# Queries and keys of retention and of two attention groups: seven block products instead of a plain product, and group-norm roots on VectorE

## The chip, the cores and the metric

The kernel runs on one core of a Trainium2 chip. The metric is the device time of one launch in microseconds. The core has TensorE (PE, matmuls out of SBUF into the eight banks of PSUM), VectorE (DVE), ScalarE (ACT), GpSimd (POOL) and SyncE (SP); SP, ACT and POOL also issue DMAs. Each engine takes its instructions in an order that is fixed when the kernel is built, and waits on semaphores for the others.

## The reference

Two decoder layers on x of 512 tokens x 1024 channels, float32. Each has a mixer and a SwiGLU feed-forward part (FFN), each followed by `x <- LayerNorm(ALPHA * x + sublayer(x))`. The mixer multiplies x by one wide matrix and splits the result:

```python
z = jnp.einsum('bsd,dc->bsc', x, w_in) + b_in
q_a, k_a, v_a, q_r, k_r, v_r, g_r, gate_a, gate_b = jnp.split(z, SPLIT_POINTS, axis=-1)
```

Attention: three groups of six heads with 64 channels, each group with its own window and dilation; scores, a position bias, a softmax, values, and a mix of the groups by their softmax denominators. Retention: four heads with queries and keys of 256 channels and values and gates of 512. Queries and keys are turned by a rotary table, and the output is normalised per token and head:

```python
return jnp.concatenate([t1 * cos - t2 * sin, t1 * sin + t2 * cos], axis=-1)   # rot(t)
return (o - mu) * lax.rsqrt(var + GN_EPS)                                      # after the scan
```

The retention output is multiplied by `silu(g_r)`; both branches are projected, weighted by sigmoid gates, summed and projected again.

## The kernel before

**Numbers in two parts.** Every float32 operand of a matmul is split into a high part (a cast on ScalarE) and a low part (the rest, a subtraction on VectorE): `hilo`, line 92. A product is then three matmuls (`mm3`, line 84): high x high, high x low, low x high. x lies transposed as `xh`, `xl` (1024 channels on 8 x 128 partitions, 512 tokens). A weight tile of 128 x 1024 is loaded into one of 8 `raw` tiles and split into `whi` and `wlo`, four of each.

**Two ways to multiply by x.** The plain way (`wstat`, line 233) holds 128 weight columns still and streams all 512 tokens: 8 x 3 matmuls of 512 columns for a result of 128 channels x 512 tokens, in one bank. The other way is a block scheme with seven products instead of eight (Winograd's form of Strassen). x is cut into channel halves and token halves, and its four sums S1 to S4 are made once per layer in `xs` (`x_sums`, line 185). Two weight matrices of equal shape stand side by side as B (columns 1 and 2, channel halves 1 and 2). Sums of B's blocks are made on the way: P1 = B11 + B12 and P3 = B12 + B22 by an accumulating DMA of POOL's queue (line 321), P2 and P4 by an addition on VectorE (line 347). `Right` (line 306) loads, sums and splits B's blocks product by product. Two routines run the seven products: `tall` (line 377; tokens on partitions, weights stream) and `wide` (line 406; channels on partitions, 256 tokens stream). In `wide` a product is 2 x 4 x 3 matmuls of 256 columns, and its results collect in three chains, a bank each: A for products 1, 6, 7 and 4, C for 5 and 3, X for 2. A function `ev` takes what is done out of the bank: after products 1, 5 and 6 a copy, after 2, 7 and 3 a sum or difference of copy and bank on VectorE, after 4 the bank itself. The FFN and the sigmoid gates use `wide`; values of attention and values with gates of retention use `tall`; queries and keys of both use the plain way.

**Order of work in a layer.** Attention has three steps `hp` (a pair of heads of each group). Step 0 makes its queries and keys along with the arrival of x. For hp = 1 and 2 a stage makes queries and keys of the three groups by `wstat` (lines 811 to 816); `qk_put` (line 712) adds the bias, scales, and writes them into a tile of the pool `opp` (nine slots), for groups 1 and 2 with the tokens reordered by dilation. Then come `rotary(0)`, the values and gates of retention head 0, and for heads 1 to 3 one after the other `rotary(h)` and `ret_values_gates(h)`. After that the sigmoid gates and the projections.

**Side work.** Small pieces of other work sit in the queue `side`. Each `mm3` of the main work gives it credit (`tick`; 0.68 for 512 columns, half of that for 256), and `pace(n)` sets the rate so that what is in the queue would be done in a credit of n. `drain` issues the rest at once. In the stage of hp the attention blocks of hp - 1 are the side work (`attention_pair`, line 513: scores, exponential, transposes, values; a block holds two banks from its scores to the copies of its values, and work tiles of a pool of six), paced to 32. In `rotary(h)` it is the outputs of head h - 1 (`ret_outputs`, line 856), in the values of h the scores of h (`ret_scores`, line 836).

**A retention head.** `rotary` (line 657) makes queries, then keys: four weight units, four banks; VectorE multiplies each bank plus bias by cos and by sin (line 668), adds and subtracts (672, 673), and `hilo` writes four tiles. `ret_outputs` takes four token blocks: matmuls, mean and variance on VectorE (868, 869), the root by `rstd_of` (line 120: a power on GpSimd and a Newton step on VectorE), a subtraction with gating (872), a scaling on ScalarE (873), then `turn`, which transposes the block and stores it.

**What sets the order.** The planner of the tile framework orders the instructions of each engine by the program's order and its own estimates: what is not ready by these is overtaken by what is, as far as free tiles and banks allow.

The functions that the change touches:

Of the kernel before, what the change touches and what calls it, by code (L numbers as in the profile page):

```python
# [12 lines left out]
F32R = mybir.dt.float32r  # L13
AF = mybir.ActivationFunctionType
# [39 lines left out]
def hybrid_kernel(ctx, tc, x, rel_bias, w_in, b_in, w_attn_proj, w_ret_proj, w_out,  # L54
# [65 lines left out]
    def rstd_of(var):  # L120
# [7 lines left out]
        dve.tensor_tensor(out=y, in0=y, in1=t, op=ALU.mult)  # L128
        return y
# [176 lines left out]
    class Right:  # L306
# [319 lines left out]
    bTs, braws = [], []  # L626
    for ly in range(DEPTH):
        bTs.append(sm.tile([P, COLS // P], F32, tag="bT", name="bT", bufs=2))
        braws.append(work("braw")[:COLS // P, :P])

    def bias_cols(ly):
# [3 lines left out]
        dve.tensor_copy(bTs[ly], px[:, :n])  # L635

    def layer(ly, cp):
# [18 lines left out]

        def rotary(h):

            rot = []
            for c0 in (C_QR + h * RQ, C_KR + h * RQ):  # L660
                us = pair_units(w_l, c0)
                prod = []
                for t in range(2):
                    ps = wstat(us, t)
                    pr = []
                    for tb in (cos, sin):
                        m = work("rp")
                        dve.scalar_tensor_tensor(out=m, in0=ps, scalar=bcol(c0 + t * P), in1=tb, op0=ALU.add, op1=ALU.mult)
                        pr.append(m)
                    prod.append(pr)  # L670
                (t1c, t1s), (t2c, t2s) = prod
                dve.tensor_tensor(out=t1c, in0=t1c, in1=t2s, op=ALU.subtract)
                dve.tensor_tensor(out=t1s, in0=t1s, in1=t2c, op=ALU.add)
                pair = []
                for src in (t1c, t1s):
                    o_ = slot("rot")
                    hilo(src, o_[:, 0], o_[:, 1])
                    pair.append(o_)
                rot.append(pair)
            heads[h]["q"], heads[h]["k"] = rot  # L680

        def ret_values_gates(h):
            cv, cg = C_VR + h * RV, C_GR + h * RV
            vr = heads[h]["v"] = [None] * NI
            gs = heads[h]["g"] = [None] * NI
            pairs = {}
# [7 lines left out]
            def gate(i, t):  # L694
                if i // 2 not in pairs:
                    pairs[i // 2] = slot("gs", F32)
                gs[i] = pairs[i // 2][:, i % 2]
# [4 lines left out]
        with stage("attn") as ap_, stage("attw", 4) as aw:  # L702
# [9 lines left out]
            def qk_put(hp, g, j, ps):  # L712
# [5 lines left out]
                dve.tensor_scalar(o_, i_, bcol(cc), (HD ** -0.5, 1.0)[j], op0=ALU.add, op1=ALU.mult)  # L718

# [115 lines left out]
        with stage("ret") as rp:  # L835
            def ret_scores(h):
# [5 lines left out]
                def one(j):  # L842
                    n = S - j * P
                    ps = psum()[:, :n]
                    for d in range(2):
                        k_, q_ = heads[h]["k"][d], heads[h]["q"][d]
                        mm3(ps, k_[:, 0, j * P:(j + 1) * P], k_[:, 1, j * P:(j + 1) * P],
                            q_[:, 0, j * P:], q_[:, 1, j * P:], d == 0, d == 1)
# [7 lines left out]
            def ret_outputs(h):  # L856

                ys = {}

                def one(i):  # L860
# [6 lines left out]
                    mv = sm.tile([P, 2], F32, tag="mv", name="mv")  # L867
                    dve.bn_stats(out=st, in_=po)
                    dve.bn_aggr(out=mv, in_=st)
                    rs = rstd_of(mv[:, 1:2])  # L870
# [335 lines left out]
```

## Time and profile before

| | |
|---|---|
| median of three runs | 2186.73 us (2182.38 to 2186.76) |
| profiled execution | 2185.52 us, span 2183.7 us |
| granted TensorE clock | 0.997 |
| busy: PE, DVE, ACT, POOL | 2161.5, 1396.0, 980.6, 228.3 us |
| DMA | 338.60 MB, 155 GB/s on average |
| attention stages hp = 1 and 2, layer 0 | about 106 to 203 us of the span |
| retention heads 1 and 2 (rotary and values), layer 0 | about 302 to 449 us |

The profile is of one execution, whose own time is 1.8 us longer than its span. A line such as `L82 PE MATMUL ps<-xs,whi 128*128 128x256 f32 x1792 | 325.7, 283 | 0.0` names the line of the kernel, engine, operation, what is written and read, the shape and the count, then the busy time in us, the mean ns of one and the idle time before them with what ended it. Matmuls overlap, so the mean of one is longer than the distance between two. `wlo` and `whi` are the parts of weights, `ps` and `px` banks, `sn` a copy of a bank.

### The profile page before, as it was taken

To read this page: it belongs to the slowest core of one execution; us is meant where nothing else is said; L and a number is where in the kernel's file an instruction comes from. 1 tells how busy PE (TensorE), PEld (TensorE's weight loads), DVE (VectorE), ACT (ScalarE), POOL (GpSimd) and SP (SyncE) were. 2 spreads that over 40 slices of the span, in tenths; PEclk is the share of its full clock that TensorE was granted. 3 is DMA by queue.
4 is the path that set the end of the run, shared out by engine and by line. 5 is a ranking of instruction groups with operands and counts; after the bars stand their busy time and mean duration, and the time that the engine had idled before them with its cause. 6 is when DMAs were issued, how large, how long until landed. Compare 5 with 4: busy or idle time off the path is not lost.

```text
span 2183.7 us, 32442 instructions
## 1 busy us (share of the span) xinstructions
PE 2161.5 (99%) x12906; PEld 1902.4 (87%) x12906; DVE 1396.0 (64%) x2011; ACT 980.6 (45%) x1585; POOL 228.3 (10%) x253
## 2 busy tenths in 40 slices
PE   8999999999999999999999999999999999999998
PEld 7977788889988899989898778888899889999996
DVE  5643677777755685747675346767877447766575
ACT  4444544546633263525245445444556233544350
POOL 4100011011000100010020000111010001000001
PEclk9999999999999999999999999999999999999999
DMA  8944266458685356656269343565577762666551
GB/s 230 235 134 104 59 164 164 135 131 194 190 305 192 88 154 132 171 133 158 93 163 255 89 92 92 140 178 148 137 188 227 260 193 58 175 151 161 125 161 39
DMA packets 304954, 338.60 MB, mean 155 GB/s; under 512 B 21790, under 2 KB 243138, under 8 KB 304673
## 3 DMA queue, kind: packets, MB, share of 16 engines
q1 hardware_dynamic: 227712, 248.81, 37.8%
q0 software_dynamic: 49808, 74.90, 18.1%
q10 hardware_dynamic: 27280, 12.80, 2.1%
q8 instruction: 101, 1.65, 0.3%
q14 instruction: 53, 0.43, 0.1%
HBM read 310.67 MB, written 28.53 MB: 155 GB/s over the span
## 4 chain that ended last, share of the span: by engine, by line
PE 90%; issue 4%; DMA 3%; DVE 2%; POOL 1%; ACT 0%; SPq 0%; POOLq 0%; DVEq 0%; ACTq 0%
PE ps L82 81%; PE px L82 7%; DMA raw<-in_w_in 2%; PE px L546 1%; DMA exd<-wb 1%; PE px L878 1%; POOL ry L125 0%; DMA mb<-exd 0%; DMA exd<-pk 0%; PE px L170 0%; DVE xtok L1001 0%; DVE wlo L336 0%; ACT whi L330 0%; PE px L602 0%; DVE xtok L1010 0%
## 5 line engine op out<-in xcount | busy, mean ns | idle before, releaser
L336 DVE TENSOR_TENSOR wlo<-raw,whi 128x1024 fp32r<-128x1024 f32 (+1 forms) x364 | 417.9, 1150 | 214.1 <-ACT whi L330 212.9
L82 PE MATMUL ps<-xh,whi 128*128 128x256 f32 (+1 forms) x1536 | 516.6, 338 | 4.5 <-ACT whi L93 3.5
L330 ACT CAST whi<-raw 128x1024 fp32r<-128x1024 f32 (+1 forms) x364 | 359.0, 990 | 345.4 <-PE ps L82 205.3
L82 PE MATMUL ps<-xh,wlo 128*128 128x256 f32 (+1 forms) x1536 | 500.9, 327 | 1.0 <-DVE wlo L94 1.0
L82 PE MATMUL ps<-xl,whi 128*128 128x256 f32 (+1 forms) x1536 | 501.2, 327 | 0.2 <-DVE xl L94 0.2
L82 PE MATMUL ps<-xs,whi 128*128 128x256 f32 (+1 forms) x2048 | 404.6, 296 | 0.0
L82 PEld LDWEIGHTS ps<-xs,whi 128*128 128x128 f32 x2048 | 327.7, 191 | 10.3
L94 DVE TENSOR_TENSOR wlo<-raw,whi 128x1024 fp32r<-128x1024 f32 (+2 forms) x162 | 193.3, 1196 | 202.0 <-ACT whi L93 201.0
L82 PEld LDWEIGHTS ps<-xh,whi 128*128 128x128 f32 x1536 | 292.4, 191 | 34.3 <-issue 5.7
L82 PEld LDWEIGHTS ps<-xh,wlo 128*128 128x128 f32 x1536 | 292.9, 191 | 26.5 <-DVE wlo L94 1.2
L82 PEld LDWEIGHTS ps<-xl,whi 128*128 128x128 f32 x1536 | 293.7, 191 | 19.5 <-DVE xl L94 1.0
L82 PE MATMUL ps<-xs,wlo 128*128 128x256 f32 (+1 forms) x1024 | 303.4, 296 | 0.0
L93 ACT CAST whi<-raw 128x1024 fp32r<-128x1024 f32 (+2 forms) x162 | 166.0, 1027 | 240.8 <-PE ps L82 150.7
L82 PE MATMUL ps<-whi,xs 128*128 128x512 f32 (+1 forms) x768 | 219.6, 360 | 0.6 <-ACT whi L330 0.4
L82 PEld LDWEIGHTS ps<-xs,wlo 128*128 128x128 f32 x1024 | 196.0, 191 | 5.0
L82 PE MATMUL ps<-whi,ht 128*128 128x512 f32 x576 | 178.4, 389 | 0.0
L82 PEld LDWEIGHTS ps<-whi,xs 128*128 128x128 f32 x768 | 137.7, 188 | 21.1 <-ACT sn L466 1.0
L82 PE MATMUL ps<-wlo,xs 128*128 128x512 f32 (+1 forms) x384 | 138.1, 360 | 0.8 <-DVE wlo L336 0.8
L321 POOL DMA_DIRECT2D raw<-in_w_in x64 | 79.2, 1263 | 472.9 <-DMA raw<-in_w_in 159.8
L82 PEld LDWEIGHTS ps<-whi,ht 128*128 128x128 f32 x576 | 108.2, 188 | 22.3
L321 POOL DMA_DIRECT2D raw<-in_w_ffn_gate x40 | 51.8, 1295 | 679.4 <-DMA raw<-in_w_ffn_up 251.4
L347 DVE TENSOR_TENSOR raw<-raw 128x1024 f32<-128x1024 f32 (+1 forms) x104 | 119.5, 1149 | 2.7 <-DMA raw<-in_w_in 0.5
(183 smaller groups left out, 2897.0 us busy)
## 6 DMA issues: line engine op xcount, KB each, us to landing
raw<-in_w_in SPq DMA_DIRECT2D x152, 512.0 KB, 4.3
raw<-in_w_ffn_up SPq DMA_DIRECT2D x64, 512.0 KB, 4.1
raw<-in_w_in POOLq DMA_DIRECT2D x48, 512.0 KB, 6.9
raw<-in_w_ffn_gate SPq DMA_DIRECT2D x44, 512.0 KB, 4.6
raw<-in_w_ffn_down SPq DMA_DIRECT2D x44, 512.0 KB, 4.2
raw<-in_w_ffn_gate POOLq DMA_DIRECT2D x40, 512.0 KB, 6.7
raw<-in_w_in SPq DMA_DIRECT2D x72, 256.0 KB, 4.9
raw<-in_w_ret_proj SPq DMA_DIRECT2D x32, 512.0 KB, 6.1
```

The costliest lines, as they stand in the source:

```text
L82: pe.matmul(ps, lhsT=a, rhs=b, start=start, stop=stop, skip_group_check=True)
L93: act.copy(out=hi, in_=src)
L94: dve.tensor_tensor(out=lo, in0=src, in1=hi.bitcast(F32), op=ALU.subtract)
L321: pool.dma_start(r, self.src({"P1": "B12", "P3": "B22"}[n], u), accum_op=ALU.add)
L330: act.copy(out=h, in_=src)
L336: dve.tensor_tensor(out=l, in0=src, in1=h.bitcast(F32), op=ALU.subtract)
L347: dve.tensor_tensor(out=r, in0=r, in1=self.t["B22" if n == "P2" else "B21", u], op=ALU.add)
L546: pe.transpose(px[:, (2 + j) * P:(3 + j) * P], s[:, hh, j * P:(j + 1) * P], ident)
L878: pe.transpose(px[:, t * P:(t + 1) * P], ys[i][:, t * P:(t + 1) * P], ident)
```

## The change

Three parts.

1. **Retention heads 1 to 3.** `rotary` uses one `wide` call: the queries' 256 columns are B's first half, the keys' the second. `biased_copy` (ScalarE, two pieces of 256 tokens, with the bias) takes out products 1, 5, 6 (negated) and 4; VectorE joins after 2, 7 and 3. `turned` multiplies a half of 256 tokens by sin and cos, adds and subtracts, and `hilo` writes it. The four rotary tiles now hold a high or a low part each and are taken from the pool at the start, as are the two of the gates. Head 0 stays plain.
2. **Group-norm roots.** The four blocks of a head collect their variances in one tile, and `rstd_vector` makes the four roots at once on VectorE (a first guess from the number's bits, three Newton steps, twelve instructions); the power on GpSimd is gone from here. The blocks' matmuls and the roots stay in the rotary of the next head (`pace(18)`), the transposes move to that head's values, in front of its scores.
3. **Attention, hp = 1 and 2.** Group 2's queries and keys come first, the plain way; then `qk_group` makes those of groups 0 and 1 in one `wide` call (B's halves: queries and keys of both groups). Its loads are split in two pieces, as the columns lie apart, and so are its accumulating DMAs. ScalarE, not VectorE, adds the bias and writes into the tiles, with the queries' bias scaled beforehand (`bQs`).

```diff
     def load(src, a, b):
         v = view(raw(), a, b)
-        nc.sync.dma_start(v, src)
+        for v_, s_ in pieces(v, src):
+            nc.sync.dma_start(v_, s_)
         return v
+
+    def pieces(v, src):
+        if len(src.shape) == 3:
+            return [(v, src)]
+        n = src.shape[3]
+        return [(v[:, :, g * n:(g + 1) * n], src[:, :, g]) for g in range(src.shape[2])]
...
+    def rstd_vector(var, n):
+        ve, y, t, u = (sm.tile([P, n], F32, tag=f"nr{i}", name="nr", bufs=2) for i in range(4))
+        dve.tensor_scalar(ve, var, EPS, None, op0=ALU.add)
+        dve.tensor_scalar(y.bitcast(I32), ve.bitcast(I32), -0.5, 1597463007.0, op0=ALU.mult, op1=ALU.add)
+        dve.tensor_scalar(ve, ve, -0.5, None, op0=ALU.mult)
+        for _ in range(3):
+            dve.tensor_tensor(out=t, in0=y, in1=y, op=ALU.mult)
+            dve.tensor_tensor(out=u, in0=t, in1=ve, op=ALU.mult)
+            dve.scalar_tensor_tensor(out=y, in0=u, scalar=1.5, in1=y, op0=ALU.add, op1=ALU.mult)
+        return y
...
                     if n in ("P1", "P3"):
-                        pool.dma_start(r, self.src({"P1": "B12", "P3": "B22"}[n], u), accum_op=ALU.add)
+                        for r_, s_ in pieces(r, self.src({"P1": "B12", "P3": "B22"}[n], u)):
+                            pool.dma_start(r_, s_, accum_op=ALU.add)
...
+        def turned(t, ts_, hi, lo):
+            n = t.shape[2]
+            s = view(work("rs"), 2, n)
+            cs, sn_ = (a[:, ts_].unsqueeze(1).to_broadcast([P, 2, n]) for a in (cos, sin))
+            dve.tensor_tensor(out=s, in0=t, in1=sn_, op=ALU.mult)
+            dve.tensor_tensor(out=t, in0=t, in1=cs, op=ALU.mult)
+            dve.tensor_tensor(out=t[:, 0], in0=t[:, 0], in1=s[:, 1], op=ALU.subtract)
+            dve.tensor_tensor(out=t[:, 1], in0=t[:, 1], in1=s[:, 0], op=ALU.add)
+            hilo(t, hi[:, :, ts_], lo[:, :, ts_])
+
         def rotary(h):
+            cq, ck = C_QR + h * RQ, C_KR + h * RQ
+            for n_ in "qk":
+                heads[h][n_] = [slot("rot") for _ in range(2)]
+            if h == 0:
...
+                return
+            sn = {}
+
+            def biased_copy(ps, c, sign=1.0):
+                o_ = view(work("sn"), 2, 256)
+                for q in range(2):
+                    act.activation(out=o_[:, q], in_=ps[:, q * 256:(q + 1) * 256], func=AF.Identity, bias=bcol(c + q * P), scale=sign)
+                return o_
+
+            def ev(i, ps):
+                p2 = ps.rearrange("p (q t) -> p q t", q=2)
+                if i in (1, 5):
+                    sn[i] = biased_copy(ps, cq if i == 1 else ck)
+                elif i == 6:
+                    sn[i] = biased_copy(ps, ck, -1.0)
+                elif i == 2:
+                    dve.tensor_tensor(out=sn[1], in0=p2, in1=sn[1], op=ALU.add)
+                    turned(sn[1], slice(0, 256), *heads[h]["q"])
+                elif i == 7:
+                    dve.tensor_tensor(out=sn[5], in0=sn[5], in1=p2, op=ALU.subtract)
+                    turned(sn[5], slice(256, 512), *heads[h]["k"])
+                elif i == 3:
+                    dve.tensor_tensor(out=sn[6], in0=p2, in1=sn[6], op=ALU.add)
+                    turned(sn[6], slice(0, 256), *heads[h]["k"])
+                elif i == 4:
+                    turned(biased_copy(ps, cq), slice(256, 512), *heads[h]["q"])
+
+            wide(pair_right(w_l[:, :, cq:], w_l[:, :, ck:], 0), x_left, ev)
...
+            def qk_group(hp):
+                def src(b, u):
+                    k = 4 if b[1] == "2" else 0
+                    c = (C_KA if b[2] == "2" else C_QA) + hp * P
+                    return w_l[:, k:k + 4, c:c + 2 * GW].rearrange("p k (g c) -> p k g c", g=2)[:, :, :, :P]
+
+                sn = {}
+
+                def put(v, j, half):
+                    for g in range(2):
...
+                        act.activation(out=o_, in_=i_, func=AF.Identity, bias=bs[:, c:c + 1], scale=(HD ** -0.5, 1.0)[j])
+
+                def ev(i, ps):
+                    p2 = ps.rearrange("p (q t) -> p q t", q=2)
+                    if i in (1, 5, 6):
+                        sn[i] = view(work("sn"), 2, 256)
+                        act.copy(out=sn[i], in_=p2)
+                    elif i == 2:
+                        dve.tensor_tensor(out=sn[1], in0=p2, in1=sn[1], op=ALU.add)
+                        put(sn[1], 0, 0)
...
+                wide(Right(src, [(4, 256)], WIDE, ("B11", "P1", "B22", "P3", "B21")), x_left, ev)
...
                 if hp:
                     for g in range(NG):
+                        qk_slot(hp, g)
+                    for g in range(2, NG):
                         us = qk_units(hp, g)
-                        qk_slot(hp, g)
                         for j in range(2):
                             qk_put(hp, g, j, wstat(us, j))
+                    qk_group(hp)
                     drain()
...
-                    rs = rstd_of(mv[:, 1:2])
...
-                    act.mul(out=y, in_=y, mul=rs)
+                def norms():
+                    rs = rstd_vector(mv[:, :, 1], NI)
+                    for i in range(NI):
+                        act.mul(out=ys[i], in_=ys[i], mul=rs[:, i:i + 1])
...
-                return ops[:1] + n * 2 + ops[1:2] + n * 2 + ops[2:3] + tr[:1] + n * 2 + ops[3:] + tr[1:2] + n * 3 \
-                    + tr[2:3] + n * 4 + tr[3:]
+                return ops[:1] + n * 2 + ops[1:2] + n * 2 + ops[2:3] + n * 3 + ops[3:] + n + [norms] + n, \
+                    n * 2 + tr[:1] + n + tr[1:2] + n + tr[2:3] + n + tr[3:]

             for h in range(RH):
                 if h:
-                    pace(20)
+                    side.extend(ops)
+                    pace(18)
                     rotary(h)
                     drain()
                     vg = ret_values_gates(h)
-                side.extend([nothing] * (8 if h else 1) + ret_scores(h))
+                    side.extend(turns + [nothing] * 2)
+                side.extend([nothing] + ret_scores(h))
                 pace(14 if h == 0 else 30)
                 run(vg)
                 drain()
-                side.extend(ret_outputs(h))
+                ops, turns = ret_outputs(h)
+            side.extend(ops + turns)
```

More of the change, by code (lines that the diff above doesn't have):

```diff
@@ L13 @@
 F32R = mybir.dt.float32r
+I32 = mybir.dt.int32
 AF = mybir.ActivationFunctionType
@@ L635, in bias_cols @@
         dve.tensor_copy(bTs[ly], px[:, :n])
+        act.mul(out=bQs[ly], in_=px[:, C_QA // P:C_QA // P + NQ], mul=HD ** -0.5)
     def layer(ly, cp):
@@ L655, in slot @@
             return opp.tile([P, 2, S], dt, tag="op", name=name)
-        def rotary(h):
[L659 to L680, printed above, removed]
+        def turned(t, ts_, hi, lo):
[7 more added lines that the diff above has]
+            hilo(t, hi[:, :, ts_], lo[:, :, ts_])
@@ L684, in ret_values_gates @@
             vr = heads[h]["v"] = [None] * NI
-            gs = heads[h]["g"] = [None] * NI
-            pairs = {}
+            pairs = [slot("gs", F32) for _ in range(2)]
+            gs = heads[h]["g"] = [pairs[i // 2][:, i % 2] for i in range(NI)]
             def left(i, ps, s):
@@ L858, in ret_outputs @@
                 ys = {}
+                mv = sm.tile([P, NI, 2], F32, tag="mv4", name="mv", bufs=2)
                 def one(i):
```

50 lines of the change are left out of this document (40 added, 10 removed).

## The prediction

> **What bounds the kernel now.** I read the page first: busy shares, then the chain of work that ended last.
>
> ```profile
> PE 2161.5 (99%) x12906; PEld 1902.4 (87%) x12906; DVE 1396.0 (64%) x2011; ACT 980.6 (45%) x1585; POOL 228.3 (10%) x253
> ...
> PE 90%; issue 4%; DMA 3%; DVE 2%; POOL 1%; ACT 0%; SPq 0%; POOLq 0%; DVEq 0%; ACTq 0%
> ```
>
> TensorE is 99% busy and 90% of the chain, so the time is the sum of its matmuls plus a few waits. A busy TensorE row says nothing of the pace, so I took the pace of the two shapes that the change exchanges: the chain inside one retention head (a pure run of 512-column matmuls, the shape of the plain product), and VectorE's timeline and TensorE's row of a stretch in the FFN (pure block products with 256 columns, where the same eviction comes back once per call of `wide`).
>
> ```profile
> 391.13 25.52 PE ps L82 x112
> ```
>
> ```profile
> 857.33 0.69 DVE L1098 TENSOR_TENSOR sn<-ps,sn 128x512 f32<-128x512 f32 x1 [0.65 <-PE ps L82]
> ...
> 877.49 0.69 DVE L1098 TENSOR_TENSOR sn<-ps,sn 128x512 f32<-128x512 f32 x1 [0.65 <-PE ps L82]
> ```
>
> ```profile
> core 0: us, PE busy (x) PEld busy (x) DVE busy (x) ACT busy (x) POOL busy (x), PEclk, DMA share, GB/s
> 877.56:897.72 20.16, 20.16 (x171) 20.16 (x170) 15.14 (x17) 10.90 (x15) 2.56 (x2) 1.00 0.79 183
> 106.00:203.00 97.00, 96.43 (x554) 76.23 (x553) 38.41 (x106) 43.21 (x146) 5.77 (x8) 1.00 0.47 123
> 302.00:449.00 147.00, 147.00 (x678) 122.15 (x677) 106.48 (x163) 68.52 (x94) 15.43 (x19) 1.00 0.58 149
> ```
>
> A 512-column matmul costs 25.52 / 112 = 0.228 us. One call of `wide` takes 877.49 - 857.33 = 20.16 us; by the code it is 7 products x 8 x 3 = 168 matmuls, so 0.120 us each (not half of 0.228). In that stretch TensorE never stopped, with VectorE at 75%. The last two rows are the stages that change: two attention stages (hp = 1 and 2 of layer 0, 48.5 us each: VectorE 40%, ScalarE 45%) and two retention heads (73.5 us each: VectorE 72%).
>
> **What it takes from TensorE.** A plain `rotary` is 2 x 2 x 8 x 3 = 96 matmuls of 512 columns: 96 x 0.228 = 21.88 us. As one `wide` it is 20.16 us, 1.72 less. Two groups' queries and keys in an attention stage are also 96, and also become one `wide`. Heads 1 to 3 of two layers are 6 places, hp = 1 and 2 of two layers are 4: 10 x 1.72 = 17.2 us. Scores, outputs, values and transposes stay the same in number; transposes only move from the next head's rotary to its values.
>
> **What it adds to VectorE in a retention head.** The prices are groups by form; the last is of the heads' window.
>
> ```profile
> L336 DVE TENSOR_TENSOR wlo<-raw,whi 128x1024 fp32r<-128x1024 f32 x308 | 375.8, 1222 | 188.0 <-ACT whi L330 187.2
> ...
> L347 DVE TENSOR_TENSOR raw<-raw 128x1024 f32<-128x1024 f32 x88 | 107.4, 1220 | 1.8
> ...
> L718 DVE TENSOR_SCALAR qk<-ps,bT 128x512 f32<-128x512 f32 x36 | 27.0, 749 | 45.0 <-PE ps L82 44.2
> ...
> L668 DVE SCALAR_TENSOR_TENSOR rp<-ps,bT,cos 128x512 f32<-128x512 f32 x32 | 23.9, 746 | 11.0 <-PE ps L82 11.0
> ...
> L872 DVE SCALAR_TENSOR_TENSOR yb<-px,mv,gs 128x512 f32<-128x512 f32 x32 | 23.7, 740 | 0.0
> ...
> L868 DVE BATCH_NORM_STATS2 st<-px 128x6 f32<-128x512 f32 x32 | 22.2, 693 | 13.9 <-PE px L82 13.9
> L94 DVE TENSOR_TENSOR rot<-rp,rot 128x512 fp32r<-128x512 f32 x32 | 20.8, 676 | 1.9 <-ACT rot L93 1.9
> ...
> L672 DVE TENSOR_TENSOR rp<-rp 128x512 f32<-128x512 f32 x16 | 10.9, 684 | 0.0
> ...
> L126 DVE SCALAR_TENSOR_TENSOR rt<-ry,ve 128x1 f32<-128x1 f32 x48 | 10.4, 219 | 43.1 <-POOL ry L125 42.8
> ...
> L128 DVE TENSOR_TENSOR ry<-ry,rt 128x1 f32<-128x1 f32 x48 | 7.5, 158 | 1.3
> ...
> L127 DVE TENSOR_SCALAR rt<-rt 128x1 f32<-128x1 f32 x48 | 7.2, 151 | 1.2
> ...
> L850 DVE TENSOR_TENSOR pt<-px,dec 128x256 f32<-128x256 f32 x8 | 3.3, 415 | 0.0
> ...
> L869 DVE BATCH_NORM_AGGREGATE mv<-st 128x2 f32<-128x6 f32 x7 | 1.3, 179 | 0.2
> ```
>
> Removed: 4 lows x 1.222, 8 bias-and-turn x 0.746, 4 sums x 0.684, 4 lows x 0.676 = 16.3 us. Added: 7 lows x 1.222, 2 sums for P2 and P4 x 1.220, 3 joins x 0.684, and 4 `turned` of 2 x 0.684 + 2 x 0.415 + 0.676 = 2.87: together 8.55 + 2.44 + 2.05 + 11.50 = 24.5 us. Roots: four times 2 x 0.151 + 0.219 + 0.158 = 0.68, that is 2.7 us, go; twelve small ones on four columns come, about 3 x 0.151 + 6 x 0.158 + 3 x 0.219 = 2.1. The Pool power leaves this place, and with it VectorE's waits behind L125; TensorE did not stand in them, so I count them as nothing. Net +7.6 us a head: 53.2 + 7.6 = 60.8 of 71.8 us, 85%, above the 75% at which the FFN runs without a wait.
>
> Inside the rotary it is tighter. VectorE has 24.5 + outputs 4 x (0.693 + 0.179 + 0.740) = 6.4 + roots 2.1 = 33.0 us, while TensorE has 20.16 + 30 output matmuls x 0.228 = 27.0 us: 6.0 us too many. Three things take that up. The values that follow leave VectorE room. The seven weight lows need nothing of the evictions, and run ahead as far as four weight buffers go: the weight casts before them wait mostly for TensorE to give a buffer back (next fence, L330). Most of the 11.5 us of `turned` falls due only with the scores, late in the values. What can be late is the first pair of lows of the values, 2 x 1.222: between 0 (the FFN's stretch) and 2.4 us a head. I take 0.5, nearer the FFN since its order of work is the same: 6 x 0.5 = 3.0 us.
>
> **ScalarE, and the attention stages.**
>
> ```profile
> L330 ACT CAST whi<-raw 128x1024 fp32r<-128x1024 f32 x308 | 321.6, 1048 | 302.4 <-PE ps L82 178.3 <-issue 63.1 <-DVE raw L347 40.7
> ...
> L1096 ACT COPY sn<-ps 128x512 f32<-128x512 f32 x60 | 34.9, 582 | 4.4 <-PE ps L82 4.4
> ...
> L927 ACT ACTIVATE sb<-sn,bT 128x256 f32<-128x256 f32 x32 | 14.5, 500 | 9.4 <-DVE sn L938 7.3 <-DVE sn L941 2.1
> ```
>
> In a rotary ScalarE gains 3 casts and 8 biased copies, 3 x 1.048 + 8 x 0.500 = 7.1 us, to (34.3 + 7.1) / 71.8 = 58%: free. An attention stage loses 4 casts and 4 evictions of VectorE, and gains 7 casts, 3 copies and 8 biased copies: ScalarE + 3 x 1.048 + 3 x 0.582 + 8 x 0.500 = + 8.9, to 30.5 of 46.8 us (65%); VectorE - 4 x 1.222 - 4 x 0.749 + 7 x 1.222 + 2 x 1.220 + 3 x 0.690 = + 5.2, to 52%. No engine is full there; the waits are in the chain of an attention block (scores, exponential, transposes, copies, values), which shares ScalarE's queue with those casts. Two resources get scarce. Of 8 PSUM banks three blocks in flight hold 6, and `wide` holds two chains and for a while a third: 9. Of 6 work tiles the group keeps 3 for sums. And the side work runs by a credit of 10.9 + 19.0 = 29.9 us where it is paced for 32, so about 3 of some 40 entries are left for the `drain` at the end. The largest stall of TensorE in such a stage today is this one (TensorE's timeline, layer 1):
>
> ```profile
> 1277.24 0.40 PE L82 MATMUL ps<-xh,wlo 128*128 128x512 f32 x1
> 1279.63 1.10 PE L82 MATMUL px<-v,sT 128*128 128x64 f32 x8 [2.00 <-ACT sT L547]
> ...
> 1281.03 0.63 PE L82 MATMUL ps<-xl,whi 128*128 128x512 f32 x1
> 1281.46 0.63 PE L82 MATMUL ps<-xh,wlo 128*128 128x512 f32 x1
> ```
>
> ```profile
> 1280.00:1284.00 4.00, 4.00 (x15) 3.24 (x15) 2.76 (x9) 1.27 (x3) 0.00 (x0) 0.58 0.07 3
> ```
>
> ```profile
> PE px L82 <- ACT sT L547: 2.6, 2, 2.0
> PE px L546 <- ACT s L538: 1.6, 1, 1.6
> ```
>
> It lost 1279.63 - 1277.24 - 0.23 = 2.2 us, and then matmuls came every 0.43 us instead of 0.228, at a granted clock of 0.58 over 4 us (second fence): 8 of them in 3.4 us, 1.6 us more, so 3.8 us. The waits over the whole span (third fence: total, times, longest) have it beside only two others behind an attention block, of 0.6 and 1.6 us. So the added wait of an attention stage lies between a gain of 0.9 (a share of that stall goes, 3.8 / 4) and a loss of 3.8 us. I take 1.0, nearer to no change, because three such waits in four stages and two first heads are all there are today: 4.0 us in all.
>
> [...]
>
> **DMA.** Each new place moves 5 loads and 2 accumulating ones of 512 KB instead of 4 loads, 1.5 MB more, 15 MB on 338.
>
> ```profile
> raw<-in_w_in SPq DMA_DIRECT2D x152, 512.0 KB, 4.3
> raw<-in_w_in POOLq DMA_DIRECT2D x48, 512.0 KB, 6.9
> raw<-in_w_in SPq DMA_DIRECT2D x72, 256.0 KB, 4.9
> ```
>
> P1 needs 4.3 + 6.9 = 11.2 us before its cast. Eight raw tiles let it start in the stage before, as in the FFN row above at a DMA share of 0.79; the stages here have 0.47 and 0.58. In the attention the pieces double the issues (10 on SP, 4 on Pool, for 8 on SP). Without cover, `wide`'s second product would wait 11.2 - 2.9 = 8.3 us; I count 0.
>
> **Sum.** - 17.2 + 3.0 + 4.0 = - 10.2 us. The profiled execution took 2185.52 us (span 2183.7), 1.2 under the median 2186.73 and inside the three runs: 2185.5 - 10.2 = 2175.3, I say 2175 us. Its own range is 2169 (no waits added, 2168.3) to 2182.
>
> **Rivals.**
> 1. The attention stages give their part back: blocks wait for banks and ScalarE, each stage takes the 3.8 us or somewhat more, so - 17.2 + 3 + 15 = + 1, or a few us under before: 2182 to 2191. For it: 9 banks wanted of 8, and the chain above. Against: the order of work is made with these limits known, and it can put a block later.
> 2. VectorE becomes the bound of the retention, and the kernel is slower. Place: the change from rotary to values in heads 1 to 3. If the low parts of the values' first weights stay behind the rotary's evictions in VectorE's order, the 6.0 us too many are TensorE's wait at each head: 6 x 6.0 = 36, so 2185.5 - 17.2 + 36 + 4 = 2208 us. It decides from 17.2 / 6 = 2.9 us a head. For it: 33.0 against 27.0 us. Against: 85% over the whole head, and four buffers of lead.
> 3. Narrow matmuls cost exactly half of wide ones in these stages: 168 x 0.114 = 19.2, 2.7 us a place, so 2185.5 - 27.4 + 7 = 2165 us. The FFN's 0.120 speaks against it. [...]
> 4. It doesn't do what it says: P1 comes late in the attention, 4 x 8.3 = 33 us lost, 2208 us again.
>
> **How the numbers follow.** The forecast has 0.52, rival 1 0.22, rival 2 0.15, rival 3 0.05, rival 4 0.06. A measurement of this kernel tells 0.2% (4.4 us) from no change: faster is below 2182.3, slower above 2191.1. Faster: 0.52 + 0.05 + 0.07 of rival 1 = 0.64; same: 0.15 and 0.03 of the milder rivals 2 and 4 = 0.18; slower 0.18. The range from 2167 to 2192 leaves out the slower cases and half of rival 3.
>
> **What would show it.** TensorE: 96 x 10 matmuls of 512 columns become 168 x 10 of 256, 13,626 in all, at 0.120 us. A retention head takes about 72.3 us instead of 73.5, an attention stage about 47.8 instead of 48.5. VectorE's busy time rises by about 6 x 7.6 + 4 x 5.2 = 66 us, ScalarE's by 78. A wait of TensorE for a low part at the start of the values beyond 2.9 us a head would show rival 2; gaps in front of transposes or values of attention, or a `wide` product held by a bank, rival 1; TensorE waiting for the cast of P1, rival 4.

## The result, and the profile after

| | before | after |
|---|---|---|
| median of four runs | 2185.64 us (2182.38 to 2186.76) | 2219.39 us (2214.42 to 2224.22) |
| ratio after / before | | 1.0152, 95% interval 1.0136 to 1.0168 |
| profiled execution, span | 2183.7 us | 2222.3 us |
| mean granted TensorE clock | 0.997 | 0.988 |
| busy: PE, DVE, ACT | 2161.5, 1396.0, 980.6 us | 2164.5, 1450.5, 1049.8 us |

The change makes the kernel 33.8 us slower; forecast was 2175 us, with a range up to 2192 us. The profiled execution of the changed kernel is the longest of its four (2224.22 us), so sums over its trace are larger than the difference of the medians. First the page of the changed kernel: busy times, and the shares of the chain of work that ended last.

```profile
PE 2164.5 (97%) x13626; PEld 1938.9 (87%) x13626; DVE 1450.5 (65%) x2067; ACT 1049.8 (47%) x1709; POOL 245.9 (11%) x249
...
PE 83%; DMA 6%; DVE 4%; issue 4%; ACT 1%; SPq 1%; POOL 0%; POOLq 0%; ACTq 0%; DVEq 0%
```

The 13,626 matmuls are as predicted. But TensorE's share of the span fell from 99% to 97%, its share of the chain from 90% to 83%, and what took its place there is DMA (3% to 6%) and VectorE (2% to 4%). No engine is anywhere near full beside TensorE. So the loss is waiting, not work. The view of TensorE's waits (what it waited for, us in total, times, longest) says where:

```profile
PE px L983 <- ACT yb L978: 18.0, 6, 3.1
PE px L569 <- ACT s L561: 17.3, 4, 6.8
PE px L83 <- ACT sT L570: 6.3, 3, 3.2
```

Before, the largest waits of this kind were 2.6 and 1.6 us in total. Three groups are new or have grown:

- L983, the transposes of a retention head's normed outputs, which the change moved into the next head's values: 6 waits of 3 us, one for each changed head of two layers.
- L569, the transposes of the softmax weights of an attention block: 4 waits, two in each layer.
- the products of those weights with the values: 3 waits, beside the same attention stages.

For sizes by stage I took TensorE's timeline. "Attention" is from the first attention-score matmul to the first retention-score matmul of a layer (stages hp = 1 and 2, head 0's rotary and values), "retention" from there to the first projection matmul, "a head" from the first score matmul of head 1 to that of head 2, layer 0.

| us, layers 0 / 1 | attention | retention | a head |
|---|---|---|---|
| before | 169.3 / 170.2 | 323.9 / 323.8 | 73.5 |
| after | 181.8 / 186.4 | 330.3 / 330.1 | 75.1 |

So attention lost 12.5 and 16.2 us, retention 6.4 and 6.3 us, 41.4 in all; the profiled spans differ by 38.6, so the rest of the kernel is 2.8 us shorter. Both stages were forecast to gain.

**A head's wait, in four timelines of the changed kernel.** Start, duration, engine, line, operation, tiles; a bracket is the idle time before it and what ended it. TensorE, at the start of the values of head 2 of layer 0 and of head 3:

```profile
411.37 0.39 PE L83 MATMUL ps<-whi,xl 128*128 128x512 f32 x1
414.73 0.66 PE L983 MATMUL px<-ident,yb 128*128 128x128 f32 x4 [2.97 <-ACT yb L978]
...
486.45 0.39 PE L83 MATMUL ps<-whi,xl 128*128 128x512 f32 x1
489.95 0.55 PE L983 MATMUL px<-ident,yb 128*128 128x128 f32 x3 [3.11 <-ACT yb L978]
```

VectorE, just before: the first root instruction, one from the middle, and the last of the chain of twelve (`nr`), between others.

```profile
403.01 0.16 DVE L144 TENSOR_SCALAR nr<-mv 128x4 f32<-128x4 f32 x1
403.08 1.22 DVE L359 TENSOR_TENSOR wlo<-raw,whi 128x1024 fp32r<-128x1024 f32 x1
...
406.92 0.16 DVE L149 TENSOR_TENSOR nr<-nr 128x4 f32<-128x4 f32 x1
407.00 1.22 DVE L359 TENSOR_TENSOR wlo<-raw,whi 128x1024 fp32r<-128x1024 f32 x1
...
413.31 0.15 DVE L150 SCALAR_TENSOR_TENSOR nr<-nr 128x4 f32<-128x4 f32 x1
```

ScalarE, which scales the blocks with these roots:

```profile
413.43 0.62 ACT L94 CAST vr<-sn 128x512 fp32r<-128x512 f32 x1 [2.25 <-DVE sn L753]
413.96 2.56 ACT L978 ACTIVATE yb<-yb,nr 128x512 f32<-128x512 f32 x4
```

The twelve instructions are 12 x 0.16 = 1.9 us of work, but each waits for the one before and stands in VectorE's order behind pieces of 0.4 to 1.2 us: the chain took 413.31 + 0.15 - 403.01 = 10.4 us. ScalarE scales the first block from 413.96, and TensorE, whose transposes of it are third in the side work of the values, stands from 411.76 to 414.73. What comes after the transposes in TensorE's order stands behind them.

**An attention stage's two waits.** TensorE in stage hp = 1 of layer 0 (first two rows), and at the end of hp = 2 (last two):

```profile
108.73 0.40 PE L83 MATMUL ps<-xh,wlo 128*128 128x512 f32 x1
113.88 0.86 PE L569 MATMUL px<-ident,s 128*128 128x128 f32 x2 [4.74 <-ACT s L561]
...
213.12 0.40 PE L83 MATMUL ps<-xh,wlo 128*128 128x512 f32 x1
216.70 1.12 PE L83 MATMUL px<-v,sT 128*128 128x64 f32 x4 [3.19 <-ACT sT L570]
```

The first: SP issues the pieces of the block product's weights from 90.67 (two of B11, then P1's first at 92.73), GpSimd the accumulating DMA of P1 from 98.73; ScalarE casts the sum, and VectorE takes the low part, the sum P2, and only then the softmax of the block (`s`, L559). The rows of SP's queue, GpSimd, ScalarE and VectorE:

```profile
90.67 5.68 SPq L112 DMA_DIRECT2D raw<-in_w_in  x6
```

```profile
92.73 0.92 SPq L112 DMA_DIRECT2D raw<-in_w_in  x1
```

```profile
98.73 2.70 POOL L344 DMA_DIRECT2D raw<-in_w_in  x2 [19.13 <-ACT sn L880]
```

```profile
109.53 1.04 ACT L353 CAST whi<-raw 128x1024 fp32r<-128x1024 f32 x1 [9.54 <-DMA raw<-in_w_in]
```

```profile
110.60 1.22 DVE L359 TENSOR_TENSOR wlo<-raw,whi 128x1024 fp32r<-128x1024 f32 x1 [9.66 <-ACT whi L353]
111.86 1.22 DVE L370 TENSOR_TENSOR raw<-raw 128x1024 f32<-128x1024 f32 x1
113.00 0.28 DVE L559 CUSTOM_DVE_ANT_0 s<-px,bias 128x128 f32<-128x128 f32 x1
```

From the first issue to the cast it took 18.9 us, from P1's own first issue 109.53 - 92.73 = 16.8 us. ScalarE and VectorE had been idle for 9.5 us before these. VectorE's softmax at 113.00 has no idle time before it, so it waited for its turn behind the low part and the sum, not for its scores. The DMA view of 92 to 110 us (KB each, median us from issue to landing) has the plain loads at 6.1 us and the accumulating ones at 9.3, against 5.3 for the plain pieces of this size in the same stretch of the kernel before:

```profile
raw<-in_w_in SPq DMA_DIRECT2D x14, 256.0 KB, 6.1
...
raw<-in_w_in POOLq DMA_DIRECT2D x4, 256.0 KB, 9.3
```

The 16 DMA engines were full in that stretch before the change too. These are the queues of the two views, first before, then after (packets, MB, share of 16 engines; packet times are added up, so a share can pass 100%):

```profile
q1 hardware_dynamic: 9630, 5.25, 104.2%
```

```profile
q1 hardware_dynamic: 7841, 4.26, 86.3%
q0 software_dynamic: 1448, 0.72, 31.9%
```

So P1's two steps, load and accumulation, were put where plain loads already took all the engines' time.

And after each of the four stops TensorE runs slow. Four stretches around them, each long enough to hold all of the slow time (busy time and instructions of PE, PEld, DVE, ACT, POOL; granted clock; DMA share; GB/s):

```profile
108.00:120.00 12.00, 7.26 (x24) 4.71 (x23) 7.27 (x17) 5.67 (x18) 0.00 (x0) 0.72 1.10 251
212.00:230.00 18.00, 13.91 (x57) 9.64 (x57) 4.94 (x13) 5.53 (x19) 1.19 (x1) 0.62 0.49 98
1206.00:1220.00 14.00, 7.16 (x24) 4.61 (x24) 7.26 (x17) 6.96 (x19) 1.30 (x1) 0.76 1.09 241
1316.00:1332.00 16.00, 11.19 (x46) 7.85 (x45) 4.80 (x13) 5.10 (x17) 1.19 (x1) 0.68 0.48 93
```

The lost clock is at most 12 x 0.28 + 18 x 0.38 + 14 x 0.24 + 16 x 0.32 = 18.7 us, an upper bound since a part of the slow time lies within the stops. So the bill is - 17.2 saved, + 18.0 + 17.3 + 6.3 of waits, - 4.2 for the waits of this kind that were there before, and + 18.7 at most for the clock: at most 38.9 us, where the profiled executions are 38.6 apart. The lower clock behind two of the heads' waits (338 to 342 us, clock 0.57, and 1440 to 1445, clock 0.66) adds 1.7 us each, and what is counted twice takes something off. So waits and lost clock make up the loss.

### The profile page after: what moved, and what is told of

Same layout as the page of the kernel before. It is cut to its first block, busy times and chain, and to the rows that moved or that the text cites. A ratio compares the mean times of both kernels' runs of the same rounds, so it can differ in the third digit from the quotient of the medians.

```text
span 2222.3 us, 34158 instructions
## 1 busy us (share of the span) xinstructions
PE 2164.5 (97%) x13626; PEld 1938.9 (87%) x13626; DVE 1450.5 (65%) x2067; ACT 1049.8 (47%) x1709; POOL 245.9 (11%) x249
## 4 chain that ended last, share of the span: by engine, by line
PE 83%; DMA 6%; DVE 4%; issue 4%; ACT 1%; SPq 1%; POOL 0%; POOLq 0%; ACTq 0%; DVEq 0%
PE ps L83 74%; PE px L83 7%; DMA raw<-in_w_in 3%; DVE wlo L359 1%; DMA exd<-wb 1%; PE px L569 1%; PE px L983 1%; DMA fa<-exd 1%; DVE rot L95 0%; POOL ry L134 0%; DMA mb<-exd 0%; PE px L192 0%; DVE xtok L1109 0%; ACT whi L94 0%; DMA exd<-pk 0%
## 5 line engine op out<-in xcount | busy, mean ns | idle before, releaser
L359 DVE TENSOR_TENSOR wlo<-raw,whi 128x1024 fp32r<-128x1024 f32 (+1 forms) x434 | 503.5, 1162 | 317.3 <-ACT whi L353 309.6
L353 ACT CAST whi<-raw 128x1024 fp32r<-128x1024 f32 (+1 forms) x434 | 433.4, 1000 | 481.6 <-PE ps L83 263.6
L83 PE MATMUL ps<-xs,whi 128*128 128x256 f32 (+1 forms) x2688 | 526.5, 294 | 0.0
L83 PE MATMUL ps<-xh,whi 128*128 128x256 f32 (+1 forms) x1456 | 456.2, 315 | 4.5 <-ACT whi L94 3.4
L83 PE MATMUL ps<-xh,wlo 128*128 128x256 f32 (+1 forms) x1456 | 444.6, 306 | 1.2 <-DVE wlo L95 1.2
L83 PE MATMUL ps<-xl,whi 128*128 128x256 f32 (+1 forms) x1456 | 445.2, 306 | 0.2 <-DVE xl L95 0.2
L83 PEld LDWEIGHTS ps<-xs,whi 128*128 128x128 f32 x2688 | 428.0, 191 | 14.2 <-issue 2.0
L83 PE MATMUL ps<-xs,wlo 128*128 128x256 f32 (+1 forms) x1344 | 393.8, 293 | 0.0
L83 PEld LDWEIGHTS ps<-xs,wlo 128*128 128x128 f32 x1344 | 257.1, 191 | 5.0
L95 DVE TENSOR_TENSOR wlo<-raw,whi 128x1024 fp32r<-128x1024 f32 (+2 forms) x122 | 144.5, 1186 | 170.1 <-ACT whi L94 170.1
```

What stands on the lines that cost most here:

```text
L83: pe.matmul(ps, lhsT=a, rhs=b, start=start, stop=stop, skip_group_check=True)
L95: dve.tensor_tensor(out=lo, in0=src, in1=hi.bitcast(F32), op=ALU.subtract)
L353: act.copy(out=h, in_=src)
L359: dve.tensor_tensor(out=l, in0=src, in1=h.bitcast(F32), op=ALU.subtract)
```

## The experiments

**Which part loses.** e1 is the changed kernel with the attention's queries and keys plain again; e2 is the kernel before with the attention part alone.

```diff
 e1, from the changed kernel
                     for g in range(NG):
-                        qk_slot(hp, g)
-                    for g in range(2, NG):
                         us = qk_units(hp, g)
+                        qk_slot(hp, g)
...
-                    qk_group(hp)
```

> The change without its attention part (queries and keys of attention made the plain way, as before). Theory: the two parts lose apart from each other, and of the 38.6 us that the span grew, the retention holds about 6.4 a layer (one wait of 3.1 us for the normalised outputs in each of heads 1 to 3, less 1.7 a head of matmul time). Expected: 2185.6 + 13 = 2198 us, with six waits of TensorE for the transposes of the outputs. Rival: the retention stages are slow only because the attention before them ended late and left work in the queues: then this runs at 2176 to 2186 us and the waits are gone.

> The kernel before with the attention part of the change alone (group 2 plain, then groups 0 and 1 in one block product; rotary, roots and outputs as before). Theory: the losses add up, attention holds 12.5 and 16.3 us by the first scores of retention: 2185.6 + 27 = 2213 us, with waits of 3 to 7 us in front of transposes of the exponentials. Rival: it loses only in company with the retention part; then it stays under 2190 us.

Measured: e1 2199.26 us, ratio 1.0059 (1.0042 to 1.0077); e2 2205.96 us, 1.0084 (1.0065 to 1.0102). Over the kernel before on the same chip (2185.75) that is + 13.5 and + 20.2 us, together 33.7 of 33.8: both parts lose, and within the intervals they add up. e2 lost 7 us less than was expected of it, e1 came out as expected. In the waits of TensorE, e1 keeps the six of the transposes, and e2 the four of the attention:

```profile
PE px L981 <- ACT yb L976: 17.9, 6, 3.0
```

```profile
PE px L555 <- ACT s L547: 16.9, 4, 4.9
```

**Is it the order, or VectorE's capacity?** e3 leaves every instruction as it is and puts the first transpose six entries later in the side work of the values.

```diff
 e3, from the changed kernel
-                    n * 2 + tr[:1] + n + tr[1:2] + n + tr[2:3] + n + tr[3:]
+                    n * 8 + tr[:1] + n + tr[1:2] + n + tr[2:3] + n + tr[3:]
```

> The whole change, with the transposes of a head's outputs six empty entries later in the side work of the values (8 instead of 2 ahead of the first). Theory: VectorE is only late with the roots, by some 3 us when the first transpose comes, and has room afterwards; so the waits of 3.1 us go at all six heads and nothing takes their place: 2219.4 - 19 = 2200 us. Rival: VectorE is the bound of the retention head; then the wait goes elsewhere (to low parts of weights), and the time stays at 2214 to 2222 us.

Measured: 2194.22 us, ratio 1.0034 (1.002 to 1.0048), 25.2 us under the changed kernel. All six waits at the transposes are gone, retention takes 319.1 us in both layers, a head 71.9. VectorE's work is the same, so its capacity was not the bound: rival 2's mechanism falls, for TensorE waits for no low part of the values here. That is 6 us better than expected, as not all of the 25.2 us is the heads' (2 x 11.1 us by the stages): the attention is shorter too, 178.6 / 180.6 us, with no edit there. It goes with a higher clock: the mean is 0.992 in the profiled execution of e3 (0.993 in e4 below) and was 0.988; why is open.

**The roots where they were.** e4 takes the roots of each block on GpSimd again, as in the kernel before; the transposes stay where the change put them.

```diff
 e4, from the changed kernel, in one(i) and norms()
+                    rs = rstd_of(mv[:, i, 1:2])
...
+                    act.mul(out=y, in_=y, mul=rs)
...
                 def norms():
-                    rs = rstd_vector(mv[:, :, 1], NI)
-                    for i in range(NI):
-                        act.mul(out=ys[i], in_=ys[i], mul=rs[:, i:i + 1])
+                    pass
```

> The whole change with the roots as before: one a block, the power on GpSimd, each scaled at once, in place of the twelve instructions for four blocks. The transposes stay where the change put them. Theory: the twelve dependent small instructions, spread in VectorE's order among others of 0.4 to 1.2 us, are what is late (10 us from the first to the last); block by block the first root is there long before the first transpose: the six waits shrink under 1 us each, 2219.4 - 15 = 2204 us, less what VectorE loses in waits for GpSimd. Rival: the evictions of the block product alone make VectorE late; then the waits stay at 2 us or more, 2215 to 2225 us.

Measured: 2191.71 us, ratio 1.0024 (1.0014 to 1.0034), 12 us better than expected and again with a shorter attention; the six waits are gone here too, retention 318.9 / 319.0, a head 71.9. So either end of the dependence cures it: earlier roots (e4) or later transposes (e3). What remains above the kernel before is the attention's, 178.1 / 176.5 us:

```profile
PE px L569 <- ACT s L561: 18.1, 4, 6.2
```

e5 to e9 start from e4.

**The retention part alone.** e5 is e4 with the attention plain (the edits of e1 and e4).

> Retention part with the roots as before (one a block, power on GpSimd), attention the plain way. Theory: the losses of the two parts add up (13.5 + 20.2 us measured apart, 33.7 together), so this is the kernel e4_pool_roots (2191.7) less the 20.2 us of the attention part: 2171.5 us, 14 under before, with no wait of TensorE in heads 1 to 3. Rival: the block product's evictions on VectorE eat part of the 1.7 us a head, and it ends at 2180 to 2186 us.

Measured: 2172.86 us against 2182.91, ratio 0.9958 (0.9944 to 0.9972). This beats both kernels. The chain of waits shows a head without a stop, 383.50 - 311.54 = 71.96 us from one run of matmuls to the same run of the next head:

```profile
311.54 11.64 PE ps L83 x71
...
383.50 11.64 PE ps L83 x71
```

Against 73.5 us before that is 1.5 less, where 1.72 was worked out; six places by 1.72 are 10.3 us, and 2182.91 - 2172.86 = 10.05 were measured. By the interval, the gain lies between 6.1 and 12.2 us. The saving on TensorE was right, and so, within that, was its size.

**P1, the first wait of the attention.** e6 leaves the accumulating DMAs of `qk_group` out, and so computes other sums (P1 is B11 alone, P3 is B12 alone); e7 computes what it should, and loads B11 and P1 before group 2's weights.

```diff
 e6, from e4: Right(..., acc=False) for qk_group, and in load()
-                    if n in ("P1", "P3"):
+                    if n in ("P1", "P3") and self.acc:
```

```diff
 e7, from e4, in qk_group and the stage
-                wide(Right(src, [(4, 256)], WIDE, ("B11", "P1", "B22", "P3", "B21")), x_left, ev)
+                right = Right(src, [(4, 256)], WIDE, ("B11", "P1", "B22", "P3", "B21"))
+                right.load("B11", "P1")
+                return lambda: wide(right, x_left, ev)
...
+                    group = qk_group(hp)
                     for g in range(2, NG):
...
-                    qk_group(hp)
+                    group()
```

> The kernel e4_pool_roots, with the accumulating DMAs of the attention's block product left out (P1 is B11 alone, P3 is B12 alone, so these queries and keys are not the reference's); their matmuls, casts and sums all stay. Theory: the first wait of each layer, 4.8 and 6.6 us at the start of stage hp = 1, comes from P1 that lands late (load, then accumulation) and holds up the attention's softmax behind its cast and its sums in the queues of ScalarE and VectorE: it goes, and with it the half clock after it, 2191.7 - 15 = 2177 us; the wait at the end of hp = 2 (4.7 and 3.6 us) stays or shrinks a little. Rival (PSUM banks and work tiles, or ScalarE's load): nothing there changes, and the time stays at 2188 to 2193 us.

> The kernel e4_pool_roots, with the loads of B11 and P1 of the attention's block product issued before those of the third group. Theory: P1 lands about 3 us earlier (four DMA issues on SP of 0.6 to 0.9 us each), the first wait of each layer falls to about 2 and 4 us, 2191.7 - 6 to 9 = 2183 to 2186 us, unless the third group's own weights then come late. Rival (banks, ScalarE): no change, 2188 to 2193 us.

Measured: e6 2178.84 us, 0.9975 (0.9965 to 0.9985); e7 2183.42 us, 1.0002 (0.9992 to 1.0012). TensorE's waits in e6, then in e7:

```profile
PE px L570 <- ACT s L562: 8.9, 2, 4.5
```

```profile
PE px L569 <- ACT s L561: 10.6, 4, 5.4
```

(The expectations' 4.8, 4.7, 6.6 and 3.6 us count from the start of the matmul before each stop; TensorE's idle times in e4 are 4.4, 4.3, 6.2 and 3.2.) In e6 the two first waits are gone and the two at the third pair are left, 4.5 and 4.4 us. In e7 the first ones shrink from 4.4 and 6.2 us to 1.0 and 1.2, with the sums computed in full, and attention takes 172.9 / 169.6 us. Each over the kernel before beside it (2185.75 for e4, 2182.91 for e6 and e7), e4 stands at + 6.0 us, e6 at - 4.1 and e7 at + 0.5: without the accumulations the kernel gains 10.0 us, and moving two loads ahead gives 5.5 of them. So the first wait is P1's lateness. What makes P1 late, the second step or the full DMA engines, these two runs do not separate, since e6 takes away both the step and its traffic.

**Banks.** e8 lets two attention blocks be in flight instead of three, which frees two banks.

```diff
 e8, from e4
-        order = ((0, scores), (2, values), (1, turn)) if hp < 2 else ((1, turn), (0, scores), (1, values))
+        order = ((0, scores), (2, values), (1, turn)) if hp < 0 else ((1, turn), (0, scores), (1, values))
```

> The kernel e4_pool_roots, with the attention blocks of all three steps in the order that the third has already: two blocks in flight instead of three, so 4 banks instead of 6. Theory of late DMAs: the waits of 4.8, 4.7, 6.6 and 3.6 us stay, 2188 to 2196 us (a little more, since less is in flight). Rival (nine banks wanted of eight, and six work tiles): the waits go, and it falls to 2172 to 2180 us.

Measured: 2193.02 us, 1.0049 (1.0034 to 1.0064), + 10.1 us where e4 stands at + 6.0, and the four waits are there:

```profile
PE px L569 <- ACT s L561: 17.2, 4, 7.1
```

This order also has less in flight, so the run alone is not clean. But e6 and e9 (below) leave banks and work tiles as they are, and there the first and the second waits are gone; so neither half of rival 1's reason (nine banks wanted of eight, six work tiles) is a cause by itself.

**The second wait.** At the third pair, TensorE waits for a block whose VectorE and ScalarE queues stand behind the exchange of softmax weights through memory (`exd`, `fa`). In the changed kernel, VectorE's row there, and ScalarE's, whose copy of the weights is what TensorE waited for at 216.70 and stands behind ScalarE's own issue of the read of `fa` (216.00):

```profile
218.33 0.69 DVE L620 TENSOR_TENSOR y<-y,fa 128x512 f32<-128x512 f32 x1 [8.99 <-DMA fa<-exd]
```

```profile
216.38 0.43 ACT L570 COPY sT<-px 128x128 f32<-128x128 f32 x2 [6.35 <-DMA exd<-wb]
```

The DMA views of the kernel before and the changed one: the write of 4 KB took 4.9 us before, and 10.3 after. (In layer 1 it is the read that grew, from 2.9 to 6.9 us.)

```profile
exd<-wb ACTq DMA_DIRECT2D x1, 4.0 KB, 4.9
...
fa<-exd ACTq DMA_DIRECT2D x1, 4.0 KB, 2.6
```

```profile
exd<-wb ACTq DMA_DIRECT2D x1, 4.0 KB, 10.3
```

In that stretch GpSimd's accumulating loads of head 0's values run. Before the change the next of them was issued at 207.79, after the exchange of 200.12 to 207.6; now two are issued at 205.73 and 208.65, beside the write of 205.65. The share of the DMA engines was 0.15 at 200 to 205 us before, and 1.10 at 211 to 216 after. e9 leaves out those of head 0's values and gates, and so computes other values and gates for this head.

```diff
 e9, from e4
             right = halves(w_l, 0, (2, 2), cv, cg, RV)
+            right.acc = h > 0
```

> The kernel e4_pool_roots, with the accumulating DMAs left out in the values and gates of retention head 0 alone (P1 is B11, P3 is B12 there, so that head's values are not the reference's). Theory: the second wait of each layer (4.7 and 3.6 us, where the third attention pair begins) comes from the exchange of softmax weights through memory, whose last small DMA takes 5.6 to 7.4 us because these accumulations run at the same time, where it takes about 3 in the kernel before; VectorE waits for it with the next block's scores behind it. Then it lands in about 3 us, the two waits fall under 2 us, and the time is 2191.7 - 6 to 10 = 2182 to 2186 us; the first waits (4.8 and 6.6) stay. Rival: the exchange begins later for other reasons (more of ScalarE's work ahead of it), and the waits stay at 3 to 5 us: 2188 to 2194 us.

Measured: 2177.99 us against 2182.7, 0.9975 (0.9966 to 0.9985). Read of `fa` in e4, then in e9, and TensorE's waits of e9:

```profile
fa<-exd ACTq DMA_DIRECT2D x1, 4.0 KB, 7.4
```

```profile
fa<-exd ACTq DMA_DIRECT2D x1, 4.0 KB, 2.9
```

```profile
PE px L571 <- ACT s L563: 6.0, 2, 3.8
```

The second waits are gone in both layers, and attention takes 168.7 / 170.4 us. The time is below the range expected, as the first waits shrank as well: they are 2.2 and 3.8 us instead of 4.4 and 6.2, though this edit lies after them; why is open. That the accumulating DMAs and the exchange meet is shown, and that their meeting costs the second wait; which resource they share is not.

**Roots on VectorE, with time to spare.** e10 is the retention part alone with the change's own roots and e3's later transposes.

> Retention part alone with the roots on VectorE as changed, and the transposes six entries later. Theory: where nothing waits for the roots, their place costs little: 2199.3 - 25 (what the same edit gave in the whole change) = 2174 us, within 3 us of e5_ret_pool (2172.9). Rival: the twelve small instructions on a busy VectorE cost by themselves, and it stays 5 us or more above e5_ret_pool.

Measured: 2174.56 us, ratio 0.9958 (0.9945 to 0.9971), the same as e5 within the intervals. Its roots are spread as wide as in the changed kernel, 398.09 + 0.15 - 387.79 = 10.5 us, and nobody waits for them:

```profile
387.79 0.16 DVE L144 TENSOR_SCALAR nr<-mv 128x4 f32<-128x4 f32 x1
...
398.09 0.15 DVE L150 SCALAR_TENSOR_TENSOR nr<-nr 128x4 f32<-128x4 f32 x1
```

So the roots on VectorE show no cost by themselves beyond the spread of the runs, and no gain either.

## Why the prediction was wrong

- **TensorE's saving: right.** 96 matmuls at 0.228 us against 168 at 0.120 gave 1.72 us a place. Without the waits a head takes 71.9 us instead of 73.5, and the retention part alone gains 10.05 us of the 10.3 worked out. Rival 3 (half-price narrow matmuls, 2.7 us a place) falls with it. For the four attention stages no run shows the saving free of waits.
- **The retention term of 0.5 us a head: the failed step is "What can be late is the first pair of lows of the values".** I summed the roots (2.1 us busy) and took them as work to be fitted in, and let the transposes "only move"; what counted was the roots' length as a chain. A dozen dependent instructions in an ordered queue took 10.4 us, and the change had put a waiting matmul at their far end. Measured: 3.0 us a head, 18.0 in all, where 3.0 in all were forecast; e3 shows that the lows that I watched were on time. A wait beyond 2.9 us a head came at the start of the values, but for the transposes and not for a low part.
- **"Pool waits counted as nothing": right.** Giving the roots back to GpSimd (e5) shows no cost against VectorE's (e10).
- **DMA, "I count 0": the failed step of the attention.** I reckoned 11.2 us from the load of P1 to its cast, and took eight raw tiles as the cover. It was 16.8 us, from 92.73 to 109.53: the prices of 4.3 and 6.9 us are medians of the whole kernel, and here loads took 6.1 and accumulations 9.3. The share of 0.47 that stood against this is a mean over 106 to 203 us; where P1 had to come in, at 92 to 110, the kernel before already had 104.2%. Rival 4 had the place and the late P1, but not the way, and P1 stopped TensorE in two of the four stages (hp = 1): no wait of TensorE in front of `wide`'s second product shows in the trace. ScalarE and VectorE stand with the late cast and its low part at the head of their queues, and the attention blocks behind them, so TensorE stood at the transposes of a block. e6 (no accumulation) and e7 (earlier) show it.
- **Attention, "+ 1.0 a stage": too small, and its reason was another.** I bounded it by today's one stall, 3.8 us, as if the change could only add stalls of the kind there were. A layer's attention took 12.5 and 16.2 us longer instead of 1.4 shorter (3.4 saved, 2.0 of waits): 9.5 and 14.1 us of waits in the two layers, and the lower clock behind them (0.62 to 0.76 in the four stretches above). Of rival 1 the "chain of an attention block" is right and the banks (e6, e8, e9) are not. The added load on the exchange of softmax weights (4.9 to 10.3 us) I did not foresee at all.
- **The rivals.** Rivals 2 and 4 named the two places where time was lost, at 2208 us each. The measured 2219 is a loss at both, which no rival had; and neither was lost in the way that its rival said.
- **Busy times.** VectorE rose by 54.5 us (66 forecast), ScalarE by 69.2 (78). Both forecasts were near enough, and neither sets the time.

## What to carry to other kernels

Cost a chain of small dependent instructions by its time from first to last in a busy ordered queue, not by its sum (10.4 us against 1.9 here): then ask what is ordered behind its last link. Putting that later was enough here (e3), and so was a shorter chain per block (e4). Cost a transfer by when it can be issued, by how full the DMA engines are in just that stretch and not in the mean (104.2% against a share of 0.47 here), and by who stands in front of whom in the queues of the engines that take it up: here the cast of the late P1 began at 109.53, and a softmax that does not use it came behind its low part and sum at 113.00. And when one change has parts, time each alone: here the retention part gains 10 us once its roots are early enough (e5), which was hidden under its own waits (e1) and under the attention part, which loses 20 (e2).

## What the runs showed of the hardware that was not expected

- **A short stop was sometimes followed by a lower clock and sometimes not.** Two of the heads' stops are of the same length. That of 2.97 us up to 414.73 was followed by a clock of 1.00; the other (row below) by 0.53 (windows of 2 us, same columns as above):

```profile
338.12 1.12 PE L983 MATMUL px<-ident,yb 128*128 128x128 f32 x4 [2.97 <-ACT yb L978]
```

```profile
414.70:416.70 2.00, 1.97 (x11) 1.67 (x12) 1.64 (x2) 2.00 (x4) 0.00 (x0) 1.00 0.00 0
...
338.00:340.00 2.00, 1.88 (x7) 1.69 (x8) 1.73 (x2) 2.00 (x5) 0.00 (x0) 0.53 0.00 0
```

  So in these traces the length of a stop does not by itself tell what the clock does after it: two stops of 2.97 us were followed by 1.00 and by 0.53, and in the kernel before a stop with 2.00 us idle was followed by 0.58 over 4 us (1280 to 1284). What decides it, no run here tests.

- **Accumulating DMAs took twice the engine time of plain ones.** In 47 us around the second wait of e4 (queue: packets, MB, share of 16 engines):

```profile
q0 software_dynamic: 1088, 2.10, 29.6%
q1 hardware_dynamic: 2320, 3.87, 27.1%
```

  That is 14.1% per MB for the queue with the accumulations (GpSimd's), against 7.0% for the plain one. At 92 to 110 us of the changed kernel (above) it is 44% against 20%. It is not GpSimd's queue as such: two plain loads of that queue, alone at 750 to 758 us of the kernel before, took 33.4% of 8 us for 1.05 MB, which is 5.4% of 47 us per MB.
